# Hymba block on one NeuronCore: gate products a chunk ahead, VectorE's extra work behind the level copies, the output gate beside the square, other fillers

## The chip, the cores and the metric

The kernel runs on one NeuronCore of a Trainium2 chip. Its engines are TensorE (PE in the profile, its weight loads PEld), VectorE (DVE), ScalarE (ACT) and GpSimd (POOL); every transfer is issued from SyncE's queue (SP). The metric is device time in microseconds of one launch. Before the change the median of three runs is 1251.34 us (1251.17 to 1252.57).

## The reference, cut to what matters

One layer runs over 1024 tokens (and 16 meta tokens ahead of them) of width 1024: a norm, one input projection, three head groups side by side (stick-breaking attention, a Mamba-2 SSD, HGRN2), an output projection, and a squared-ReLU MLP. The change concerns the two recurrent groups, which the reference runs in chunks of 128 tokens:

```python
def ssd step(state, inp):                      # per chunk, 8 heads of 64
    decay = masked_decay(acum_t - acum_s)      # exp, causal
    y_diag = einsum('btsh,bshp->bthp', (c_c b_c) * decay, x_c)
    y_off  = einsum('bthn,bhpn->bthp', c_h, state) * exp(acum)
    state  = state * exp(acum[-1]) + einsum('bshn,bsh,bshp->bhpn', b_h, w_end, x_c)
    ...
def hgrn2 step(S, inp):                        # per chunk, 4 heads of 64
    gcum = cumsum(g_c, axis=1)                 # g = log forget gate, per channel
    scores  = einsum('bthk,btshk,bshk->btsh', q_c, masked_decay(gcum_t - gcum_s), k_c)
    o = einsum('btsh,bshv->bthv', scores, v_c) + einsum('bthk,bhkv->bthv', q_c * exp(gcum), S)
    S = S * exp(gcum[-1]) + einsum('bshk,bshv->bhkv', k_c * exp(gcum[-1] - gcum), v_c)
...
o = rmsnorm(o, out_norm) * silu(g)             # the output gate
h = h + concat([o_sb, o_ssd, o_hg]) @ w_out
```

## The kernel before

The launch has four stretches: the input projection and attention (to about 388 us of the profiled execution), chunks 1 to 8 of the two recurrences (to about 621 us), and the MLP as two levels of block products, to the end.

The function chunk(c, steps, per) does one chunk. HGRN2's scores are not made with logarithms but in seven levels, block sizes b = 1, 2, 4, ... 64. The tile qb holds the queries, kx the keys (cx in the profile, one ring of buffers), f4 the forget gates, S the scores (a5 or wT, read as a). In level b hg_levels issues on TensorE two products of all keys with the later half of each block pair's queries (pa<-qb,cx; four records in the profile); on VectorE the multiplication of that query half by the gate product of the earlier half (qb<-qb,f) and a predicated copy of the new scores into S; on GpSimd the multiplication of the earlier key half by the gate product of the later half (cx<-cx,f), and then the product of the pairs of gates, in place, as the gates of the next level (f<-f). Level b+1's score product therefore waits for both halves. In even chunks the query and gate tiles are slices of one g buffer, so the names there are g<-g,g and cx<-cx,g.

Between the levels stands the SSD's work: on VectorE two scans of the decay (levels 1 and 2), y = state output by decay (wT<-mq,cwt, third level), the decays times c b (k<-pb,k, 128x512 each, fourth and fifth), and the scaling of the state (sst<-sst,tot); on GpSimd the 128x512 products a<-a,dtt (third level), a<-a,dbc (fourth), wT<-wT,a (fifth) and a<-a,cwt (sixth).

TensorE is filled up with the products of the output projection of the chunk before, out_steps(c-1), 48 matmuls of 128x512 in two halves (mf<-g,wsA or wsB): take(steps, per) issues per of them after each level, one after the diagonal product (pb<-a,k), and what is left ahead of the transposes at the chunk's end. Chunk 1 fills with work of the gates (ig_all), chunk 8 with the output projection of chunk 7 and first products of the MLP. In chunks 3 to 6 a normalised tile of the MLP is made as well.

The chunk's end: VectorE adds the HGRN2 output (cx<-pc,cx; otf in the code), ScalarE squares it, VectorE sums (ro<-cx, a TENSOR_REDUCE), GpSimd raises the SSD's and HGRN2's mean squares to -1/2 (rr<-rr,mhalf and ro<-ro,mhalf), VectorE multiplies by it (cx<-cx,ro), GpSimd multiplies by the output gate (cx<-cx,igt), and TensorE transposes the mix: attention's part (pc<-ident,kto), the SSD's (mq<-ident,wT), HGRN2's (pc<-ident,cx). ScalarE and VectorE split that into two rounded parts for the next output projection. Then the next chunk's first level follows on TensorE.

What sets the order: a scheduler orders each engine's instructions by its own estimate; behind(i, j) adds a dependence without a semaphore, which holds i after j in the queue of one engine. lastcp is the last predicated copy, lastkv the last key product. All loads stand in one queue in the order in which SyncE issues them.

Of the kernel before, what the change touches and what calls it, by code (L numbers as in the profile page):

```python
# [15 lines left out]
P = 128  # L16
# [52 lines left out]
def tile_hybrid_block(  # L69
# [799 lines left out]
    def hg_levels(qb, kx, f4, S, levels, m):  # L869
        for b in levels:  # L870
# [38 lines left out]
    def halves(fn):  # L909
        for h in range(2):  # L910
            fn(slice(64 * h, 64 * h + 64), h)
# [55 lines left out]
    def mlp_tr(c, xn, qq=(0, 1), tag="mf"):  # L967

        off = (c - 1) * P
        for q in qq:  # L970
# [2 lines left out]
            urgent[0] = A.copy(hi, src)  # L973
            V.tensor_tensor(lo, src, hi, op=ALU.subtract)

    def chunk(c, steps, per):

        t0 = (c - 1) * P
# [6 lines left out]
        if c <= 2:
            if c == 1:
                hgt[1] = sb([4, P], "qb"), sb([4, P], "f4"), sb([4, P], "a5")
            else:
                qf = sb([G3], "g3")[:, 0:D].rearrange("p (a q t) -> p a q t", a=2, t=P)
                hgt[0] = qf[:, 0], qf[:, 1], sb([4, P], "wT")  # L990
            halves(lambda s, h: G.memset(hgt[c % 2][0][s, 1 - h::2, :], 0.0))
            G.memset(hgt[c % 2][2], 0.0)
        qb, f4, S = hgt[c % 2]
        halves(lambda s, h: SY.dma_start(qb[s, h::2, :], dr_qf[:, s, cs].rearrange("f p t -> p f t")))
        kx = sb([CU], "cu")[:, 0:256].rearrange("p (q t) -> p q t", t=P)
        SY.dma_start(kx, dr_k[:, :, cs].rearrange("f p t -> p f t"))
        for h in range(2):
            SY.dma_start(f4[:, h::2, :], dr_f[:, :, cs].rearrange("f p t -> p f t"))
        xb = sb([K4], "k4")[:, 0:D].rearrange("p (f t) -> p f t", t=P)
        SY.dma_start(xb, dr_x[:, :, cs].rearrange("f p t -> p f t"))  # L1000
        dec = sb([K4], "k4")[:, 0:D].rearrange("p (h t) -> p h t", t=P)
# [12 lines left out]
        yf = y.rearrange("p h d -> p (h d)")  # L1014
        ot = sb([3 * P], "ca")[:, 0:256].rearrange("p (h d) -> p h d", d=64)
        for n, b in enumerate(LEVELS):
            hg_levels(qb, kx, f4, S, (b,), P)
            if n <= 1:
                dg = dec[:, 4 * n:4 * n + 4, :].rearrange("p h t -> p (h t)")
                behind(V.tensor_tensor_scan(dg, dg, ident4, 0.0, ALU.mult, ALU.add), lastcp[0])  # L1020
            if n == 0:
                xt = ssd_x(xb, P)
            elif n == 1:
                bt = ssd_b(xb, P)
            elif n == 2:
                pc = ps("pb")
                for g in range(2):
                    mm(pc[:, g * P:(g + 1) * P], lhsT=xb[:, 4 + g, :], rhs=xb[:, 6 + g, :], start=True, stop=True)
                py = ps("mq")
                for g in range(2):  # L1030
                    mm(py[:, g * 256:(g + 1) * 256], lhsT=xb[:, 6 + g, :], rhs=sst[:, g * 256:(g + 1) * 256],
                       start=True, stop=True)
                V.tensor_tensor(y, py.rearrange("p (h d) -> p h d", d=64), inner(cwt[:, c, 0, :], [P, 8, 64]),
                                op=ALU.mult)
                behind(G.tensor_tensor(xd, xt, inner(dtt[:, c, :], [P, 8, 64]), op=ALU.mult), lastkv[0])
            elif n in (3, 4):
                g = n - 3
# [562 lines left out]
```

## Time and profile before

| | us |
|---|---|
| three runs, median (range) | 1251.34 (1251.17 to 1252.57) |
| the profiled execution's own time | 1251.57 |
| its span, first to last instruction | 1249.5 |
| TensorE busy, share of the span | 1209.6, 97% |
| VectorE, ScalarE, GpSimd busy | 885.8, 584.0, 429.9 |
| chunks 1 to 8, about | 388 to 621 |

The profile is of one execution of the program. A row of the timeline gives the start of an instruction, its duration, the engine, the operation with output and inputs (128x512 is partitions by elements), and in square brackets how long the engine had stood idle before it and who released it. A count (x4) says that so many alike were joined in a row. Matmuls overlap in their pipeline, so ends are modelled. PEclk, or granted clock, is the clock that the throttle gave TensorE as a share of full speed.

### The profile page before, as it was taken

What the parts mean: (1) busy time and instruction counts of PE and PEld (TensorE: products, weight loads), DVE (VectorE), ACT (ScalarE), POOL (GpSimd) and SP (SyncE); (2) the same over time, 40 slices, a digit from 0 to 9 for tenths busy, and PEclk for the clock granted to TensorE, in tenths of its full rate; (3) what the DMA queues carried; (4) which work ended last, traced back from release to release, by engine and by line L of the source; (5) the groups of instructions that cost most, each with busy time, mean ns of one, the idle gap of its engine ahead of it and who ended that gap; (6) DMA issues with size and microseconds to landing.
All of it is one profiled execution on the core that took longest, in us unless ns stands there. A gap on an engine that the chain in (4) does not pass through costs nothing.

```text
span 1249.5 us, 18592 instructions
## 1 busy us (share of the span) xinstructions
PE 1209.6 (97%) x6362; PEld 1037.4 (83%) x6362; DVE 885.8 (71%) x1449; ACT 584.0 (47%) x1237; POOL 429.9 (34%) x500
## 2 busy tenths in 40 slices
PE   7999999999999998998899999999999999999998
PEld 6989999999888777777788888888887888888887
DVE  5777877775324688887546756666998778778777
ACT  6755676664322332233355644445566444344331
POOL 4233222322102466766524555666752000000000
PEclk9999999999999989999999999999999999999999
DMA  6311112233345666463246666777766554554556
GB/s 209 94 40 46 54 39 58 71 97 99 85 118 132 177 206 133 94 121 92 70 143 188 224 210 215 241 242 245 233 210 215 174 157 138 161 152 148 163 190 211
DMA packets 195031, 184.14 MB, mean 147 GB/s; under 512 B 14405, under 2 KB 149853, under 8 KB 194938
## 3 DMA queue, kind: packets, MB, share of 16 engines
q1 hardware_dynamic: 194938, 182.97, 48.9%
q8 instruction: 50, 0.82, 0.3%
q14 instruction: 43, 0.35, 0.1%
HBM read 128.25 MB, written 54.67 MB: 146 GB/s over the span
## 4 chain that ended last, share of the span: by engine, by line
PE 78%; DVE 9%; POOL 3%; ACT 3%; issue 3%; DMA 3%; SPq 0%; POOLq 0%; ACTq 0%; DVEq 0%
PE pa L119 25%; PE mf L119 23%; PE pc L119 17%; PE mq L119 7%; PE pb L119 3%; DVE k L96 3%; DVE g L96 2%; PE pb L122 1%; POOL cx L96 1%; DVE a L96 1%; PE pa L122 1%; DVE cx L96 1%; DVE wT L96 1%; PE pc L122 1%; ACT g L96 1%
## 5 line engine op out<-in xcount | busy, mean ns | idle before, releaser
L119 PE MATMUL pa<-g,k 128*128 128x512 f32 x864 | 208.8, 389 | 0.8 <-DVE f L96 0.8
L119 PEld LDWEIGHTS pa<-g,k 128*128 128x128 f32 x864 | 162.0, 188 | 35.2 <-DVE f L96 1.2
L119 PE MATMUL mf<-g,wsA 128*128 128x384 f32 (+2 forms) x624 | 139.3, 358 | 0.0
L119 PE MATMUL mf<-g,wsB 128*128 128x384 f32 (+2 forms) x624 | 136.5, 355 | 0.0
L119 PEld LDWEIGHTS mf<-g,wsA 128*128 128x128 f32 x624 | 104.4, 190 | 6.6 <-DVE wsA L96 0.3
L119 PEld LDWEIGHTS mf<-g,wsB 128*128 128x128 f32 x624 | 103.6, 189 | 6.1
L96 DVE TENSOR_TENSOR k<-g,k 128x512 fp32r<-128x512 f32 x80 | 81.0, 1013 | 28.6 <-ACT k L96 28.0
L119 PE MATMUL mf<-g,g 128*128 128x512 f32 (+1 forms) x408 | 100.8, 394 | 0.0
L96 ACT CAST g<-cx 128x512 fp32r<-128x512 f32 x80 | 49.5, 619 | 85.8 <-DVE cx L96 59.2
L119 PEld LDWEIGHTS mf<-g,g 128*128 128x128 f32 (+1 forms) x408 | 72.5, 183 | 15.1 <-issue 0.3
L119 PE MATMUL pc<-g,k 128*128 128x512 f32 x336 | 82.5, 389 | 0.0
L96 DVE TENSOR_TENSOR g<-pa,g 128x512 f32<-128x512 f32 (+2 forms) x82 | 54.9, 679 | 38.1 <-PE pa L119 32.2
L96 POOL TENSOR_TENSOR cx<-cx 128x384 f32<-128x384 f32 (+2 forms) x34 | 38.6, 1135 | 118.7 <-ACT cx L96 78.6
L119 PEld LDWEIGHTS pc<-g,k 128*128 128x128 f32 x336 | 63.1, 188 | 13.2
L119 PE MATMUL mf<-g,k 128*128 128x512 f32 x288 | 69.6, 392 | 1.8 <-ACT a L96 1.5
L119 PE MATMUL pa<-g,st 128*128 128x512 f32 x240 | 65.1, 390 | 0.3 <-ACT g L96 0.3
L119 PEld LDWEIGHTS mf<-g,k 128*128 128x128 f32 x288 | 53.6, 188 | 13.5 <-ACT a L96 1.9
L96 DVE TENSOR_TENSOR g<-cx,g 128x512 fp32r<-128x512 f32 x80 | 60.5, 756 | 4.9 <-ACT g L96 3.5
L96 POOL TENSOR_TENSOR g<-g,g 128x512 f32<-128x512 f32 x32 | 45.7, 1436 | 49.8 <-issue 45.5
L96 ACT CAST k<-g 128x512 fp32r<-128x512 f32 x80 | 48.9, 615 | 20.2 <-PE pb L119 11.4
L119 PEld LDWEIGHTS pa<-g,st 128*128 128x128 f32 x240 | 45.0, 188 | 10.1 <-ACT g L96 0.7
L96 DVE SCALAR_TENSOR_TENSOR cx<-cx,cwb 128x384 f32<-128x384 f32 (+1 forms) x72 | 43.5, 605 | 9.2 <-ACT cx L96 8.6
(358 smaller groups left out, 2719.6 us busy)
## 6 DMA issues: line engine op xcount, KB each, us to landing
g<-in_w_up_dram SPq DMA_DIRECT2D x48, 512.0 KB, 4.9
st<-in_w_in_dram SPq DMA_DIRECT2D x51, 256.0 KB, 2.9
cx<-in_w_down_dram SPq DMA_DIRECT2D x48, 256.0 KB, 2.8
wT<-dr_s SPq DMA_DIRECT2D x45, 256.0 KB, 3.0
dr_s<-a SPq DMA_DIRECT2D x40, 256.0 KB, 2.3
g<-in_x_dram SPq DMA_DIRECT2D x16, 512.0 KB, 5.5
dr_s<-st SPq DMA_DIRECT2D x32, 256.0 KB, 2.5
a<-dr_s SPq DMA_DIRECT2D x23, 256.0 KB, 2.9
```

The lines of the kernel that those rows point to most:

```text
L96: i = fn(*a, **k)
L119: return queue(nc.tensor.matmul(*a, **k))
L122: return queue(nc.tensor.transpose(*a, **k))
```

## The change

Five things are changed in the chunks. The gates of chunk c+1 are loaded during chunk c (load_f), and their products of all levels are written to a tile of their own, fp, a chunk ahead, one level behind each key product of the running chunk (f_products); chunk 1's seven products stand before its levels, and hg_level reads f4 or fp. Three VectorE products of the SSD (y, the decays times c b, the scaling of the state) are held behind the predicated copy of their level, and the addition to the state behind the row sum. The output gate is multiplied in on GpSimd beside ScalarE's square, before the two powers, and VectorE's multiplication by the norm is the last step ahead of the transposes. Before the transposes at most 10 filler matmuls are taken instead of all that is left, so that two follow behind them; chunk 2 takes 6 per level instead of 5. The DMA scratch of the program is made smaller, which gives the room for fp.

```diff
+    def f_products(f4, fp, b):
+        v = f_level(f4, fp, b).rearrange("p q (n t) -> p q n t", t=2)
+        return G.tensor_tensor(f_level(f4, fp, 2 * b), v[:, :, :, 0], v[:, :, :, 1], op=ALU.mult)
...
+    def load_f(c):
+        cs = slice(NM + (c - 1) * P, NM + c * P)
...
+        f4 = hgt[c % 2][1]
+        for h in range(2):
+            SY.dma_start(f4[:, h::2, :], dr_f[:, :, cs].rearrange("f p t -> p f t"))
...
+        if c == 1:
+            load_f(1)
+            for b in LEVELS:
+                f_products(hgt[1][1], hgt[1][3], b)
+        qb, f4, S, fp = hgt[c % 2]
...
-        for h in range(2):
-            SY.dma_start(f4[:, h::2, :], dr_f[:, :, cs].rearrange("f p t -> p f t"))
+        if c < 8:
+            load_f(c + 1)
...
-            hg_levels(qb, kx, f4, S, (b,), P)
+            hg_level(qb, kx, f4, fp, S, n)
+            if c < 8:
+                behind(f_products(hgt[1 - c % 2][1], hgt[1 - c % 2][3], b), lastkv[0])
...
-                V.tensor_tensor(y, py.rearrange("p (h d) -> p h d", d=64), inner(cwt[:, c, 0, :], [P, 8, 64]),
-                                op=ALU.mult)
+                behind(V.tensor_tensor(y, py.rearrange("p (h d) -> p h d", d=64), inner(cwt[:, c, 0, :], [P, 8, 64]),
+                                       op=ALU.mult), lastcp[0])
...
-                V.tensor_tensor(dec[:, 4 * g:4 * g + 4, :], outer(pc[:, g * P:(g + 1) * P], [P, 4, P]),
-                                dec[:, 4 * g:4 * g + 4, :], op=ALU.mult)
+                behind(V.tensor_tensor(dec[:, 4 * g:4 * g + 4, :], outer(pc[:, g * P:(g + 1) * P], [P, 4, P]),
+                                       dec[:, 4 * g:4 * g + 4, :], op=ALU.mult), lastcp[0])
...
-        V.reduce_sum(ro[:, 0:4], sq.rearrange("p (h d) -> p h d", d=64), axis=mybir.AxisListType.X)
+        red = V.reduce_sum(ro[:, 0:4], sq.rearrange("p (h d) -> p h d", d=64), axis=mybir.AxisListType.X)
+        gated = ig[:, 256:512]
+        G.tensor_tensor(gated, otf, gated, op=ALU.mult)
...
-        V.tensor_tensor(ot, ot, inner(ro[:, 0:4], [P, 4, 64]), op=ALU.mult)
-        G.tensor_tensor(otf, otf, ig[:, 256:512], op=ALU.mult)
+        V.tensor_tensor(ot, gated.rearrange("p (h d) -> p h d", d=64), inner(ro[:, 0:4], [P, 4, 64]), op=ALU.mult)
...
-        V.tensor_tensor(s3, s3, inner(tot[:, c - 1, :], [P, 8, 64]), op=ALU.mult)
-        V.tensor_tensor(sst, pst, sst, op=ALU.add)
+        behind(V.tensor_tensor(s3, s3, inner(tot[:, c - 1, :], [P, 8, 64]), op=ALU.mult), lastcp[0])
+        behind(V.tensor_tensor(sst, pst, sst, op=ALU.add), red)
...
-        take(steps, 1000 if c < 8 else 26)
+        take(steps, 10 if c < 8 else 26)
...
-        chunk(c, under(out_steps(c - 1), wo1, 0, 5), 5)
+        chunk(c, under(out_steps(c - 1), wo1, 0, 5), 6 if c == 2 else 5)
...
-    nc = _bacc.Bacc("TRN2", target_bir_lowering=False, num_devices=1)
+    nc = _bacc.Bacc("TRN2", target_bir_lowering=False, num_devices=1, dynamic_dma_scratch_size=1024)
```

The order of VectorE in chunk 5, from the third level's query half to the fifth level's copy, is this before (qb is the query tile, a the scores, k the decays, wT the SSD's output, sst its state):

```order
L96 TENSOR_TENSOR qb_4203<-qb_4203,f_568_4204 128x64x4
L96 COPY_PREDICATED a_569_4205<-hmask,pa_5329 128x64x4
L96 TENSOR_TENSOR k_740_5279<-pb_5336,k_740_5279 128x512 x2
L96 TENSOR_TENSOR wT_5288<-mq_5339,cwt 128x512
L96 TENSOR_TENSOR sst<-sst,tot 128x512
L96 TENSOR_TENSOR qb_4203<-qb_4203,f_568_4204 128x32x8
L96 COPY_PREDICATED a_569_4205<-hmask,pa_5349 128x32x8
L96 TENSOR_TENSOR qb_4203<-qb_4203,f_568_4204 128x16x16
L96 COPY_PREDICATED a_569_4205<-hmask,pa_5371 128x16x16
L96 TENSOR_TENSOR g_749_5304<-mf_5306,g_749_5304 128x512
```

and this after:

```order
L96 TENSOR_TENSOR qb_4203<-qb_4203,fp_4206 128x64x4
L96 COPY_PREDICATED a_569_4205<-hmask,pa_5340 128x64x4
L96 TENSOR_TENSOR wT_5299<-mq_5350,cwt 128x512
L96 TENSOR_TENSOR qb_4203<-qb_4203,fp_4206 128x32x8
L96 COPY_PREDICATED a_569_4205<-hmask,pa_5360 128x32x8
L96 TENSOR_TENSOR k_742_5290<-pb_5347,k_742_5290 128x512
L96 TENSOR_TENSOR qb_4203<-qb_4203,fp_4206 128x16x16
L96 COPY_PREDICATED a_569_4205<-hmask,pa_5382 128x16x16
L96 TENSOR_TENSOR k_742_5290<-pb_5347,k_742_5290 128x512
L96 TENSOR_TENSOR g_751_5315<-mf_5317,g_751_5315 128x512
```

Between the copies of the third level and the query half of the fourth stand one product instead of four; the two decay products are behind the copies of the fourth and the fifth level, and the state's scaling stands behind the seventh level's copy.

GpSimd in the same place, from the third level's key product on (cx is the keys, a and wT the SSD's tiles), before:

```order
L96 TENSOR_TENSOR cx<-cx,f_568_4204 128x32x4
L96 TENSOR_TENSOR a_743_5286<-a_748_5302,dtt 128x512
L96 TENSOR_TENSOR f_568_4204<-f_568_4204 128x64
L96 TENSOR_TENSOR cx<-cx,f_568_4204 128x16x8
L96 TENSOR_TENSOR a_748_5302<-a_748_5302,dbc 128x512
L96 TENSOR_TENSOR f_568_4204<-f_568_4204 128x32
L96 TENSOR_TENSOR cx<-cx,f_568_4204 128x8x16
L96 TENSOR_TENSOR wT_5288<-wT_5288,a_748_5302 128x512
```

and after:

```order
L96 TENSOR_TENSOR cx<-cx,fp_4206 128x32x4
L96 TENSOR_TENSOR fp_4224<-fp_4224 128x4x16
L96 TENSOR_TENSOR a_745_5297<-a_750_5313,dtt 128x512
L96 TENSOR_TENSOR cx<-cx,fp_4206 128x16x8
L96 TENSOR_TENSOR fp_4224<-fp_4224 128x4x8
L96 TENSOR_TENSOR a_750_5313<-a_750_5313,dbc 128x512
L96 TENSOR_TENSOR cx<-cx,fp_4206 128x8x16
L96 TENSOR_TENSOR fp_4224<-fp_4224 128x4x4
L96 TENSOR_TENSOR wT_5299<-wT_5299,a_750_5313 128x512
```

The products stand in the queue as many times as before, now those of the next chunk's gates (fp_4224) and ahead of the SSD's product of the level instead of behind it; the key products read fp_4206, which the chunk before has written.

GpSimd at the end of chunk 5, from the clearing of the query tile on (rr and ro are the mean squares, igt the output gate), before:

```order
L96 MEMSET g_621_4553 64x2x128
L96 TENSOR_SCALAR rr_5205<-rr_5205 128x2
L96 TENSOR_TENSOR rr_5205<-rr_5205,mhalf 128x2
L96 TENSOR_SCALAR ro_5222<-ro_5222 128x4
L96 TENSOR_TENSOR ro_5222<-ro_5222,mhalf 128x4
L96 TENSOR_TENSOR cx<-cx,igt_5043 128x256
```

and after:

```order
L96 MEMSET g_571_4222 64x2x128
L96 TENSOR_TENSOR igt_5054<-cx,igt_5054 128x256
L96 TENSOR_SCALAR rr_5216<-rr_5216 128x2
L96 TENSOR_TENSOR rr_5216<-rr_5216,mhalf 128x2
L96 TENSOR_SCALAR ro_5233<-ro_5233 128x4
L96 TENSOR_TENSOR ro_5233<-ro_5233,mhalf 128x4
```

The gate has moved from the last place of the five to the first.

## Rows read from the trace of the kernel before

**Rows 1.** The view of the cores: span, and mean granted clock of TensorE.

```profile
core 0: 1249.5 us, clock 0.997
```

**Rows 2.** The table by stretch, of which chunk 2, chunk 5 and chunk 8 are shown: stretch and its length, busy time and instructions of PE, PEld, DVE, ACT and POOL, granted clock, DMA share, GB/s.

```profile
429.00:461.00 32.00, 26.76 (x140) 21.78 (x139) 26.21 (x43) 10.04 (x23) 18.13 (x26) 0.89 0.70 234
...
512.00:538.00 26.00, 23.70 (x146) 20.11 (x147) 21.38 (x38) 7.84 (x17) 17.79 (x28) 1.00 0.49 107
...
589.00:621.00 32.00, 28.40 (x162) 23.75 (x163) 19.84 (x35) 12.00 (x31) 18.77 (x31) 1.00 0.26 87
```

**Rows 3.** The waits of TensorE from 386 to 621 us, all chunks, without the last line of 0.3 us: what it waited for, us in total, how many times, the longest.

```profile
PE pa L119 <- DVE g L96: 5.2, 5, 1.3
PE pa L119 <- DVE qb L96: 4.6, 3, 1.9
PE pc L122 <- POOL cx L96: 3.3, 6, 0.7
PE pa L119 <- POOL cx L96: 2.8, 7, 0.5
PE pb L119 <- ACT a L96: 2.7, 1, 2.7
PE mf L119 <- ACT a L96: 1.5, 1, 1.5
```

**Rows 4.** TensorE's timeline in chunk 5 from the fourth level on (fillers and other products between are left out).

```profile
519.73 0.61 PE L119 MATMUL pa<-qb,cx 128*128 128x128 f32 x4
...
522.78 0.68 PE L119 MATMUL pa<-qb,cx 128*128 128x128 f32 x4 [1.28 <-DVE qb L96]
...
524.46 0.60 PE L119 MATMUL pa<-qb,cx 128*128 128x128 f32 x4
...
526.50 0.71 PE L119 MATMUL pa<-qb,cx 128*128 128x128 f32 x4
...
533.36 3.12 PE L119 MATMUL mf<-g,wsB 128*128 128x512 f32 x12
...
537.75 0.44 PE L122 MATMUL pc<-ident,cx 128*128 128x128 f32 x2 [0.62 <-POOL cx L96]
```

**Rows 5.** VectorE's timeline in chunk 5.

```profile
518.91 1.28 DVE L96 TENSOR_TENSOR k<-pb,k 128x512 f32<-128x512 f32 x2
520.11 0.68 DVE L96 TENSOR_TENSOR wT<-mq,cwt 128x512 f32<-128x512 f32 x1
520.70 0.75 DVE L96 TENSOR_TENSOR sst<-sst,tot 128x512 f32<-128x512 f32 x1
521.38 1.26 DVE L96 TENSOR_TENSOR qb<-qb,f 128x256 f32<-128x256 f32 x1
...
525.76 0.43 DVE L96 TENSOR_TENSOR qb<-qb,f 128x256 f32<-128x256 f32 x1 [0.63 <-POOL f L96]
...
533.02 0.42 DVE L96 TENSOR_TENSOR cx<-pc,cx 128x256 f32<-128x256 f32 x1
...
534.58 0.41 DVE L96 TENSOR_REDUCE ro<-cx 128x4 f32<-128x256 f32 x1
536.40 0.43 DVE L96 TENSOR_TENSOR cx<-cx,ro 128x256 f32<-128x256 f32 x1 [1.41 <-POOL ro L96]
```

**Rows 6.** GpSimd's timeline in chunk 5.

```profile
520.48 0.42 POOL L96 TENSOR_TENSOR cx<-cx,f 128x128 f32<-128x128 f32 x1 [0.54 <-PE pa L119]
520.87 1.49 POOL L96 TENSOR_TENSOR a<-a,dbc 128x512 f32<-128x512 f32 x1
522.72 0.31 POOL L96 TENSOR_TENSOR f<-f 128x32 f32<-128x32 f32 x1 [0.36 <-DVE qb L96]
523.61 0.66 POOL L96 TENSOR_TENSOR cx<-cx,f 128x128 f32<-128x128 f32 x1 [0.58 <-PE pa L119]
524.24 1.28 POOL L96 TENSOR_TENSOR wT<-wT,a 128x512 f32<-128x512 f32 x1
...
525.80 0.65 POOL L96 TENSOR_TENSOR cx<-cx,f 128x128 f32<-128x128 f32 x1
526.41 1.04 POOL L96 TENSOR_TENSOR a<-a,cwt 128x512 f32<-128x512 f32 x1
...
533.93 0.19 POOL L96 TENSOR_SCALAR rr<-rr 128x2 f32<-128x2 f32 x1 [1.56 <-ACT a L96]
...
535.36 1.01 POOL L96 TENSOR_TENSOR ro<-ro,mhalf 128x4 f32<-128x4 f32 x1
536.97 0.72 POOL L96 TENSOR_TENSOR cx<-cx,igt 128x256 f32<-128x256 f32 x1 [0.60 <-DVE cx L96]
```

**Rows 7.** TensorE's timeline in chunk 2, at its third level.

```profile
436.89 1.22 PE L119 MATMUL pb<-k 128*128 128x128 f32 x4 [2.71 <-ACT a L96]
...
439.90 2.69 PE L119 MATMUL mf<-g,wsA 128*128 128x512 f32 x5
...
444.94 1.40 PE L119 MATMUL mf<-g,wsA 128*128 128x512 f32 x5
```

**Rows 8.** ScalarE's timeline in chunk 2, ahead of the row of TensorE that waits.

```profile
435.04 1.33 ACT L96 ACTIVATE g<-g,nwt 128x512 fp32r<-128x512 f32 x2 [4.94 <-DMA g<-in_w_out_dram]
```

**Rows 9.** TensorE's timeline, the fifth and the seventh level of chunk 8.

```profile
599.87 0.68 PE L119 MATMUL pa<-g,cx 128*128 128x128 f32 x4 [1.29 <-DVE g L96]
...
603.60 0.71 PE L119 MATMUL pa<-g,cx 128*128 128x128 f32 x4 [0.29 <-POOL cx L96]
```

More of the change, by code (lines that the diff above doesn't have):

```diff
@@ L53 @@
 BUFS = dict(g1=4, g2=2, g3=8, wsA=1, wsB=1, k4=4, st=3, a1=1, a2=1, a3=1, a4=1, a5=1, qb=1, f4=1, wT=2,
-            igt=1, rr=6, ro=2, sm=4, sst=1)
+            igt=1, rr=6, ro=2, sm=4, sst=1, fp=2)
 PBUFS = dict(mf=2, mq=1, pa=2, pb=1, pc=2)
@@ L892, in hg_levels, with f_level, hg_level @@
                 G.tensor_tensor(fv[:, :, :, 0, 0], fv[:, :, :, 0, 0], fv[:, :, :, 1, 0], op=ALU.mult)
+    FP = {2: 0, 4: 64, 8: 96, 16: 112, 32: 120, 64: 124, 128: 126}
+    def f_level(f4, fp, b):
+        return f4 if b == 1 else fp[:, :, FP[b]:FP[b] + P // b]
+    def f_products(f4, fp, b):
+        v = f_level(f4, fp, b).rearrange("p q (n t) -> p q n t", t=2)
+        return G.tensor_tensor(f_level(f4, fp, 2 * b), v[:, :, :, 0], v[:, :, :, 1], op=ALU.mult)
+    def hg_level(qb, kx, f4, fp, S, li):
+        b = LEVELS[li]
+        n = 64 // b
+        kv, qv, sv = (t.rearrange("p q (n t b) -> p q n t b", t=2, b=b) for t in (kx, qb, S))
+        fv = f_level(f4, fp, b).rearrange("p q (n t) -> p q n t", t=2)
+        pl = ps("pa")
+        for p in range(2):
+            mm(pl[:, p * P:(p + 1) * P], lhsT=kx[:, p, :], rhs=qv[:, 2 * p:2 * p + 2, :, 1, :], start=True, stop=True)
+        lq = V.tensor_tensor(qv[:, :, :, 1, :], qv[:, :, :, 1, :], fv[:, :, :, 0:1].broadcast_to([P, 4, n, b]),
+                             op=ALU.mult)
+        msk = hmask[:, li:li + 1, :].broadcast_to([P, 4, 64]).rearrange("p q (n b) -> p q n b", b=b)
+        lastcp[0] = V.copy_predicated(sv[:, :, :, 1, :], msk, pl[:, 0:256].rearrange("p (q n b) -> p q n b", q=4, b=b))
+        behind(lastcp[0], lq)
+        lastkv[0] = G.tensor_tensor(kv[:, :, :, 0, :], kv[:, :, :, 0, :],
+                                    fv[:, 0::2, :, 1:2].broadcast_to([P, 2, n, b]), op=ALU.mult)
     def hg_tokens(kx, m):
@@ L974, in mlp_tr @@
             V.tensor_tensor(lo, src, hi, op=ALU.subtract)
+    def load_f(c):
+        cs = slice(NM + (c - 1) * P, NM + c * P)
+        if c <= 2:
+            if c == 1:
+                hgt[1] = sb([4, P], "qb"), sb([4, P], "f4"), sb([4, P], "a5"), sb([4, P], "fp")
+            else:
+                qf = sb([G3], "g3")[:, 0:D].rearrange("p (a q t) -> p a q t", a=2, t=P)
+                hgt[0] = qf[:, 0], qf[:, 1], sb([4, P], "wT"), sb([4, P], "fp")
+            halves(lambda s, h: G.memset(hgt[c % 2][0][s, 1 - h::2, :], 0.0))
+            G.memset(hgt[c % 2][2], 0.0)
+        f4 = hgt[c % 2][1]
+        for h in range(2):
+            SY.dma_start(f4[:, h::2, :], dr_f[:, :, cs].rearrange("f p t -> p f t"))
     def chunk(c, steps, per):
@@ L982, in chunk @@
         mixes[c] = mix
[L985 to L993, printed above, removed]
+        if c == 1:
+            load_f(1)
+            for b in LEVELS:
+                f_products(hgt[1][1], hgt[1][3], b)
+        qb, f4, S, fp = hgt[c % 2]
         halves(lambda s, h: SY.dma_start(qb[s, h::2, :], dr_qf[:, s, cs].rearrange("f p t -> p f t")))
@@ L1091, in chunk @@
         rms_r(ro, P, 4)
-        V.tensor_tensor(ot, ot, inner(ro[:, 0:4], [P, 4, 64]), op=ALU.mult)
-        G.tensor_tensor(otf, otf, ig[:, 256:512], op=ALU.mult)
+        V.tensor_tensor(ot, gated.rearrange("p (h d) -> p h d", d=64), inner(ro[:, 0:4], [P, 4, 64]), op=ALU.mult)
         pst = ssd_state(bt, xw, P)
         s3 = sst.rearrange("p (h d) -> p h d", d=64)
-        V.tensor_tensor(s3, s3, inner(tot[:, c - 1, :], [P, 8, 64]), op=ALU.mult)
-        V.tensor_tensor(sst, pst, sst, op=ALU.add)
+        behind(V.tensor_tensor(s3, s3, inner(tot[:, c - 1, :], [P, 8, 64]), op=ALU.mult), lastcp[0])
+        behind(V.tensor_tensor(sst, pst, sst, op=ALU.add), red)
         hv = hst.rearrange("p a h d -> p a (h d)")
-        V.tensor_tensor(hv, hv, f4[:, 0::2, 0:1].broadcast_to([P, 2, P]), op=ALU.mult)
+        V.tensor_tensor(hv, hv, fp[:, 0::2, FP[P]:FP[P] + 1].broadcast_to([P, 2, P]), op=ALU.mult)
         halves(lambda s, h: V.tensor_tensor(hst[s, :, h, :], pk[s, 0:2, h, :], hst[s, :, h, :], op=ALU.add))
-        take(steps, 1000 if c < 8 else 26)
+        take(steps, 10 if c < 8 else 26)
         p2 = ps("pc")
```

## The prediction

> **What bounds the kernel now.** First the cores: one core, 1249.5 us, granted clock 0.997 [rows 1], so nearly all of the time is at full clock, and the profiled execution of 1251.57 us is 0.23 above the median of 1251.34. Then the stretches: the change touches chunks 1 to 8 alone, and there TensorE is busy for 23.70 of 26 us in a middle chunk, VectorE for 21.38 and GpSimd for 17.79 [rows 2]. TensorE is the bound, so an edit pays only where it takes away a wait of TensorE; the fillers keep their number. The waits of TensorE over all the chunks are the ceiling: 5.2 + 4.6 + 3.3 + 2.8 + 2.7 + 1.5 = 20.1 us [rows 3], 1.6% of the time. Two groups are large: scores that wait for VectorE's query half (9.8 us in 8 waits) and the transposes at a chunk's end that wait for GpSimd's gate (3.3 in 6).
>
> The middle chunks are alike, so I walk through chunk 5, with the fourth level's scores, at 519.73, as zero. The fifth level stands at 3.05, the sixth at 4.73, the seventh at 6.77, and the last transposes at 18.02 [rows 4]. The fifth comes after a wait of 1.28. Its releaser is the query half of 1.26 us, which started at 521.38, 1.65 after the scores that let it go; ahead of it in VectorE's queue stood the two decay products (1.28 for both), y (0.68) and the state's scaling (0.75) [rows 5]. At the end GpSimd finishes the second power at 535.36 + 1.01 = 536.37, VectorE multiplies for 0.43, GpSimd puts the gate in for 0.72, and TensorE goes on at 537.75, after a wait of 0.62 [rows 4 to 6].
>
> **The change part by part. VectorE behind the copies.** Only y (0.68) is left ahead of the fourth query half; its input comes from a product ahead of the fourth scores, so it hides there. The query half then starts with its scores, and alone it takes 0.43, not 1.26 [rows 5]. Two waits are thus gone, and the fifth level can stand at 3.05 − 1.28 = 1.77, which is TensorE's own work, and the sixth at 1.77 + 1.68 = 3.45, the seventh at 3.45 + 2.04 = 5.49 by the distances of before, in which nothing waits [rows 4]. VectorE's next extras: each decay product (0.64) now follows a copy, and VectorE stood idle for 0.63 ahead of the sixth query half [rows 5]; the state's scaling (0.75) follows the seventh copy, where its hiding place is the diagonal product on TensorE. I cost these at nothing; without that cover they are rival C.
>
> **GpSimd is late next.** Its fourth key product ends at 0.75 + 0.42 = 1.17; a gate product of 0.31 follows, now ahead of the SSD's product and no longer held by VectorE (0.36 idle before); then a<-a,dbc. It took 1.49 beside the long query half; the same shape took 1.04 as a<-a,cwt [rows 6]. I take 1.04, since the query half that it ran beside moves off: 2.52. The fifth key product (0.66) ends at 3.18, ahead of the sixth scores at 3.45. Product 0.31, wT<-wT,a 1.28, key product 0.65: 5.42 [rows 6], against 5.49 on TensorE. Five joints of some 0.03 to 0.05 between instructions put it at about 5.65, so GpSimd holds the seventh level by 0.1 to 0.2: 6.77 − 5.65 = 1.1 gained, of 1.28. The third level's wait on GpSimd (within the 2.8 us of [rows 3]) I leave as it is: the products still stand between the key products there.
>
> **Gate products a chunk ahead.** They are as many and as long as before, and no longer between two levels of one chain; their gain is the 0.36 and the wait of 0.63 above, already in the sum. Chunk 8 has none to make: both its waits, 1.29 and 0.29 [rows 9], can go: 1.6. The loads move ahead in SyncE's queue by a chunk; they are small and land long before they are read.
>
> **Output gate beside the square.** From the second power on, the path is now VectorE's 0.43 and the transposes: the gate's 0.72 and a joint of some 0.1 go, 0.8 less. Paid for ahead: GpSimd's gate can start when VectorE's otf is there, 533.02 + 0.42 = 533.44, and ends at 534.16, while rr was ready at 533.93 [rows 5, 6]: 0.2 to 0.4 later for the powers that follow. Net 0.5, at most the 0.62 of the wait.
>
> **Fillers.** Two matmuls move behind the last transposes, 3.12 / 12 = 0.26 each [rows 4]. They cover nothing of TensorE ahead of the next scores, and 0.5 less cover stands ahead of the transposes; with the waits before them mostly gone I count 0.2 lost. A middle chunk so gains 1.1 + 0.5 − 0.2 = 1.4; bounds 0.6 (GpSimd at its long durations) and 2.3 (all its waits).
>
> **Chunks 1 and 2.** Here the order changes most: seven gate products of chunk 2 now stand at chunk 1's end on GpSimd, ahead of the two powers: between seven of the short row of 0.31, 2.2, and seven of the gate's 0.72, 5.0 [rows 6]; I take 3, since each is half as long as the one before; six fillers a level instead of five in chunk 2. What sets chunk 2 is another thing: its third level waits 2.71 for ScalarE [rows 7], which itself stands 4.94 for the output weights [rows 8], at 435.04. These weights' issue moves hardly, so a later end of chunk 1 is mostly absorbed. Bounds: −4 (all of the 2.7 and the first-levels' waits go) and +3 (the products come out whole). Nearest is the row that stays, the weights' landing: I take −0.5.
>
> **Sum.** Chunks 3 to 6: 4 × 1.4 = 5.6. Chunk 7, which makes no MLP tile but has the longest wait, 1.9 [rows 3]: 1.3 (its end gains less, as the next chunk's queue is shorter). Chunk 8: 1.6, and 0.3 by the gate: 1.9. Chunks 1 and 2: 0.5. Together 9.3, under half of the 20.1. The profiled execution would be 1251.57 − 9.3 = 1242.3, a median 1242.0.
>
> **The rivals. B, GpSimd becomes the pace.** a<-a,dbc stays at 1.49 instead of 1.04 and the key products at 0.66 instead of 0.42: 0.45 + 0.24 = 0.69 later in a middle chunk, of which the slack leaves 0.6. For it: the 1.49 and the 0.66 are the rows at that very place [rows 6], and VectorE stays as busy there as before, with the decays. Against it: the decay products read one input from PSUM. Then a middle chunk gains 0.8, chunk 7 0.7, chunk 8 1.4: 3.2 + 0.7 + 1.4 + 0.5 = 5.8, a time of 1245.5. Beside it stands the Trainium skill, GPSIMD Engine Reference, "8. Key points": GpSimd shares its SBUF interfaces with VectorE and contends with it when VectorE runs in a two-port mode or reads two SBUF inputs. By that rule, the trace agrees: a query half and a GpSimd product that run together took 1.26 and 1.49, apart 0.43 and 1.04.
>
> **C, slower: VectorE becomes the bound at the end.** The decays, and the state's scaling, 1.28 + 0.75, with y 0.68 2.7 in all, find no idle VectorE in the levels and come out behind the seventh copy, ahead of the additions that the diagonal product releases. It decides from the point where VectorE's idle time in levels 5 to 7 is under what was moved there. Price: 2.7 − 1.28 = +1.4 a chunk in five chunks, 7.0, less 1.9 in chunk 8 and 0.5: 1251.3 + 4.6 = 1255.9. Against it: 4.6 us of VectorE idle in a middle chunk (26 − 21.38 [rows 2]), with 0.63 ahead of the sixth query half alone.
>
> **D, the half clock of chunk 2 goes.** Five fillers took 2.69 at 439.90 and 1.40 at 444.94 [rows 7]; the mean of the stretch was 0.89 [rows 2], so 0.11 × 32 = 3.5 us were lost to 1.2 GHz after the wait of 2.71. If that wait closes, 3.5 more: 1238.5. Against it: the weights land when they landed.
>
> **E, no change to speak of.** GpSimd as in B, and chunk 2's seven products delay chunk 1's end and with it the transposes, 3 us, with nothing of it absorbed: −5.8 + 0.5 + 3 = −2.3, a time of 1249.0.
>
> **How the numbers follow.** A measurement of this kernel can tell about 0.2%, 2.5 us, from no change. Forecast 0.53 (1240 to 1244), B 0.25, D 0.07, all faster: 0.85. E 0.09: the same. C 0.06: slower. The time is the likeliest case's, 1242.0. The range reaches down to D and up to the worse end of B, and leaves out C, E and what lies beyond D, 0.2 in all: 1237.8 to 1248.3.
>
> **What would show it.** Right: in chunks 3 to 7 the fifth scores come without a wait of over 0.3, the fourth query half lasts some 0.43 and starts with its scores; the seventh scores stand about 5.6 after the fourth; the last transposes follow VectorE's cx<-igt,ro and no GpSimd row; what took 26 us in chunk 5 takes 24.6. B shows as a GpSimd row of 1.4 to 1.5 ahead of scores that wait for cx; C as a diagonal product's addition on VectorE that starts late; D as a granted clock of 1.0 in chunk 2; E as a chunk 1 that is 3 us longer. It would be wrong altogether if the scores in chunks 3 to 6 waited for something that no row here shows, such as a late load of gates.

## The result, and the profile after

| | before | after |
|---|---|---|
| median of four runs, us | 1251.95 (1251.17 to 1252.76) | 1240.29 (1239.97 to 1243.86) |
| ratio, 95% interval | | 0.9908 (0.9897 to 0.9920) |
| the profiled execution, us (span) | 1251.57 (1249.5) | 1243.86 (1242.1) |

Some 11.6 us less, 0.9%; 1242.0 was forecast, with 1237.8 to 1248.3 as the range.

The profiled execution of after is 3.5 us or more above the others: it reaches chunk 1 2.7 us later than before, in a stretch where both kernels run the same order, with 3.4 us at half clock (granted clock 0.5) near 62 us, so chunks are compared by their own lengths.

TensorE's starts of the first-level scores (the first pa<-..,cx of a chunk; chunk 8 to the first transpose pa<-ident,qb behind it) give the length of each chunk, us:

| chunk | 1 | 2 | 3 | 4 | 5 | 6 | 7 | 8 | sum |
|---|---|---|---|---|---|---|---|---|---|
| before | 38.40 | 31.76 | 25.62 | 25.83 | 25.77 | 25.80 | 25.41 | 37.28 | 235.87 |
| after | 40.33 | 29.82 | 24.22 | 24.29 | 24.27 | 24.27 | 23.33 | 35.22 | 225.75 |
| forecast of the difference | −0.5 for both | | −1.4 | −1.4 | −1.4 | −1.4 | −1.3 | −1.9 | −9.3 |
| measured | +1.93 | −1.94 | −1.40 | −1.54 | −1.50 | −1.53 | −2.08 | −2.06 | −10.12 |

The waits of TensorE from 386 to 621 us, after; they answer to [rows 3]: what it waited for, total, times, longest.

```profile
PE pa L119 <- DVE g L96: 3.4, 2, 2.0
PE pc L122 <- DVE cx L96: 2.4, 6, 0.5
PE mq L122 <- ACT wT L96: 1.7, 2, 1.2
PE mf L119 <- ACT a L96: 1.3, 1, 1.3
PE pa L119 <- POOL cx L96: 0.6, 2, 0.4
```

The 9.8 us of waits for VectorE's query half have become 3.4, in two waits, both in chunk 2. The ends of chunks still wait, now for VectorE's multiplication, 2.4 in all instead of 3.3.

TensorE's timeline in chunk 5, after, against [rows 4]: the scores of levels 4 to 7, the transposes of the MLP tile between the last two of them, the fillers and transposes at the end, and the next chunk's first scores.

```profile
519.41 0.60 PE L119 MATMUL pa<-qb,cx 128*128 128x128 f32 x4
...
521.01 0.61 PE L119 MATMUL pa<-qb,cx 128*128 128x128 f32 x4
...
522.61 0.67 PE L119 MATMUL pa<-qb,cx 128*128 128x128 f32 x4
...
523.92 0.63 PE L122 MATMUL mf<-ident,k 128*128 128x128 f32 x4 [0.17 <-DVE g L96]
...
525.09 0.61 PE L119 MATMUL pa<-qb,cx 128*128 128x128 f32 x4
...
531.84 2.66 PE L119 MATMUL mf<-g,wsB 128*128 128x512 f32 x10
...
535.53 0.44 PE L122 MATMUL pc<-ident,cx 128*128 128x128 f32 x2 [0.38 <-DVE cx L96]
535.72 0.71 PE L119 MATMUL mf<-g,wsB 128*128 128x512 f32 x2
536.27 0.62 PE L119 MATMUL pa<-g,cx 128*128 128x128 f32 x4
```

Counted from the fourth scores, the fifth stand at 1.60, the sixth at 3.20, the seventh at 5.68 (before 3.05, 4.73, 6.77; for the seventh 5.65 was forecast), the last transposes at 16.12 (18.02).

VectorE and then GpSimd in the same place, after, against [rows 5] and [rows 6].

```profile
520.05 0.43 DVE L96 TENSOR_TENSOR qb<-qb,fp 128x256 f32<-128x256 f32 x1 [0.91 <-PE pa L119]
...
523.10 0.67 DVE L96 TENSOR_TENSOR g<-mf,g 128x512 f32<-128x512 f32 x1
```

```profile
520.16 0.59 POOL L96 TENSOR_TENSOR cx<-cx,fp 128x128 f32<-128x128 f32 x1 [0.39 <-PE pa L119]
520.73 0.23 POOL L96 TENSOR_TENSOR fp<-fp 128x32 f32<-128x32 f32 x1
520.92 1.03 POOL L96 TENSOR_TENSOR a<-a,dbc 128x512 f32<-128x512 f32 x1
521.93 0.59 POOL L96 TENSOR_TENSOR cx<-cx,fp 128x128 f32<-128x128 f32 x1
...
523.90 0.58 POOL L96 TENSOR_TENSOR cx<-cx,fp 128x128 f32<-128x128 f32 x1
...
531.85 0.73 POOL L96 TENSOR_TENSOR igt<-cx,igt 128x256 f32<-128x256 f32 x1 [0.99 <-DVE cx L96]
```

The fourth query half takes 0.43 and is released by its scores, 0.64 behind their start; a<-a,dbc takes 1.03. The key products come in time: the one for the seventh scores ends at 523.90 + 0.58 = 524.48, 0.61 ahead of the scores at 525.09. What stands just ahead of those are the transposes of the MLP tile, which wait for VectorE's g<-mf,g; they start 0.89 behind the fillers in front of them, 0.55 in the kernel before.

Chunk 1's end on GpSimd, after: the products of chunk 2's gates, which start when those have landed, the gate, and the two powers behind.

```profile
425.52 1.09 POOL L96 TENSOR_TENSOR fp<-g 128x256 f32<-128x256 f32 x1 [2.85 <-DMA g<-dr_f]
426.69 1.15 POOL L96 TENSOR_TENSOR fp<-fp 128x128 f32<-128x128 f32 x3
...
428.29 0.50 POOL L96 TENSOR_TENSOR fp<-fp 128x16 f32<-128x16 f32 x2
428.75 0.73 POOL L96 TENSOR_TENSOR igt<-cx,igt 128x256 f32<-128x256 f32 x1
...
430.26 0.70 POOL L96 TENSOR_TENSOR rr<-rr,mhalf 128x2 f32<-128x2 f32 x1
430.95 1.01 POOL L96 TENSOR_TENSOR ro<-ro,mhalf 128x4 f32<-128x4 f32 x1
```

TensorE waits 1.24 there for the SSD's scaled output. In chunk 2 its third level then waits 2.04, for a query half queued behind a split of the output weights. ScalarE's first split of these starts 44.6 us behind chunk 1's first scores, in the kernel before 44.4 ([rows 8]): the weights land as late as before. The half clock in chunk 2 lasts 3.4 us instead of 6.8.

### The profile page after: what moved, and what is told of

Same layout as the page of the kernel before. It is cut to its first block, busy times and chain, and to the rows that moved or that the text cites. A ratio compares the mean times of both kernels' runs of the same rounds, so it can differ in the third digit from the quotient of the medians.

```text
span 1242.1 us, 18593 instructions
## 1 busy us (share of the span) xinstructions
PE 1210.7 (97%) x6362; PEld 1037.9 (84%) x6362; DVE 880.5 (71%) x1449; ACT 584.2 (47%) x1237; POOL 424.5 (34%) x500
## 4 chain that ended last, share of the span: by engine, by line
PE 80%; DVE 8%; issue 3%; ACT 3%; POOL 3%; DMA 3%; SPq 0%; DVEq 0%; POOLq 0%; ACTq 0%
PE pa L119 25%; PE mf L119 25%; PE pc L119 16%; PE mq L119 7%; PE pb L119 3%; DVE g L96 3%; DVE k L96 2%; PE pb L122 1%; POOL rr L96 1%; PE pa L122 1%; ACT k L96 1%; DVE cx L96 1%; DMA g<-in_x_dram 1%; DMA g<-in_w_out_dram 1%; DVE a L96 1%
## 5 line engine op out<-in xcount | busy, mean ns | idle before, releaser
L119 PEld LDWEIGHTS pa<-g,st 128*128 128x128 f32 x240 | 45.0, 188 | 10.1 <-ACT g L96 0.8
```

What stands on the lines that cost most here:

```text
L119: return queue(nc.tensor.matmul(*a, **k))
```

## The experiments

Each was timed against the kernel before on the same chip (the change in the runs above). An interval on a ratio is about 0.0013 to either side, 1.6 us; finer statements rest on the chunk lengths of the profiled execution, which mostly agree to 0.05 us between kernels with the same order in the chunk. The last two columns are such lengths, in us.

| kernel | us | ratio (interval) | chunks 3 to 6 | chunk 7 |
|---|---|---|---|---|
| before | 1251.95 to 1252.91 | 1 | 25.62 to 25.83 | 25.41 |
| the change | 1240.29 | 0.9908 (0.9897, 0.9920) | 24.22 to 24.29 | 23.33 |
| e_dve_unheld | 1244.03 | 0.9933 (0.9920, 0.9945) | 24.23 to 24.24 | 26.70 |
| e_gate_last | 1246.17 | 0.9955 (0.9942, 0.9969) | 24.61 to 24.64 | 23.72 |
| e_fillers_old | 1238.10 | 0.9891 (0.9877, 0.9904) | 23.78 to 23.80 | 22.68 |
| e_dve_only | 1246.34 | 0.9954 (0.9940, 0.9967) | 24.47 to 24.70 | 23.78 |
| e_products_only | 1241.44 | 0.9909 (0.9893, 0.9924) | 24.05 to 24.13 | 25.19 |
| e_product_behind | 1245.42 | 0.9941 (0.9929, 0.9954) | 25.02 to 25.05 | 25.36 |
| e_products2_late | 1242.37 | 0.9918 (0.9905, 0.9932) | 24.23 to 24.30 | 23.35 |
| v_splits_later | 1233.81 | 0.9854 (0.9840, 0.9867) | 23.59 to 24.14 | 22.68 |
| v_spread | 1232.75 | 0.9851 (0.9836, 0.9866) | 23.57 to 23.59 | 22.67 |
| v_spread_late2 | 1234.56 | 0.9855 (0.9839, 0.9872) | 23.58 to 24.14 | 22.66 |

**e_dve_unheld**, from the changed kernel:

```diff
-                behind(V.tensor_tensor(y, ...), lastcp[0])
+                V.tensor_tensor(y, ...)
-                behind(V.tensor_tensor(dec[:, 4 * g:4 * g + 4, :], ...), lastcp[0])
+                V.tensor_tensor(dec[:, 4 * g:4 * g + 4, :], ...)
-        behind(V.tensor_tensor(s3, ...), lastcp[0])
-        behind(V.tensor_tensor(sst, pst, sst, op=ALU.add), red)
+        V.tensor_tensor(s3, ...)
+        V.tensor_tensor(sst, pst, sst, op=ALU.add)
```

> The changed kernel with VectorE's y, decay products, state scaling and state addition not held behind the copies, so that they stand ahead of the fourth query half again; all else as changed. Theory (VectorE's order gives the levels' gain): the fifth scores wait 1.2 to 1.3 us again in chunks 3 to 8, the seventh scores stand some 6.8 after the fourth instead of 5.7; 6 x 1.1 = 6.6 us, a time near 1247. Rival (the gate products a chunk ahead give the gain): the waits stay away, 1240 to 1242.

Neither came out whole. The queue ahead of the fourth query half was the old one again, yet the wait of the fifth scores came back at 0.48 only and chunks 3 to 6 kept their length: in exchange TensorE gets back 0.4 between the sixth and the seventh scores, and the wait of 0.38 at the chunk's end is gone. TensorE, VectorE and GpSimd, chunk 5 of e_dve_unheld:

```profile
517.95 0.68 PE L119 MATMUL pa<-qb,cx 128*128 128x128 f32 x4 [0.48 <-DVE qb L96]
```

```profile
516.56 0.86 DVE L96 TENSOR_TENSOR sst<-sst,tot 128x512 f32<-128x512 f32 x1
517.35 0.46 DVE L96 TENSOR_TENSOR qb<-qb,fp 128x256 f32<-128x256 f32 x1
```

```profile
516.84 0.68 POOL L96 TENSOR_TENSOR fp<-fp 128x32 f32<-128x32 f32 x1
517.49 1.22 POOL L96 TENSOR_TENSOR a<-a,dbc 128x512 f32<-128x512 f32 x1
```

The query half starts 0.14 ahead of a<-a,dbc and takes 0.46. In chunk 7, where one more VectorE instruction stands ahead of it, it comes second:

```profile
566.47 1.26 DVE L96 TENSOR_TENSOR qb<-qb,fp 128x256 f32<-128x256 f32 x1
```

```profile
565.96 1.48 POOL L96 TENSOR_TENSOR a<-a,dbc 128x512 f32<-128x512 f32 x1
```

There it takes 1.26, TensorE waits 1.93, and chunk 7 has 3.4 us at half clock just behind: 26.70 against 23.33. In these profiles that is more than the whole difference of the chunks, 2.8. Part of it can be the half clock of this execution: one execution of e_dve_unheld had a mean clock of 1.000 and took 1241.39, and the one of the change with that clock 1240.21.

**e_dve_only**: the kernel before with the lines just shown as + put in as they stand in the change, no more.

> The kernel before with only VectorE's three extras held behind the copies (and the state's addition behind the row sum); gate products in place, gate last, fillers as before. Theory: the fifth scores' wait goes and GpSimd with its products in place is just in time for the sixth and the seventh: 1.0 to 1.2 a chunk in six chunks, 6 to 7 us, a time of 1245 to 1246. Rival (without the products a chunk ahead GpSimd holds the sixth and seventh scores, so the order of VectorE alone brings little): the seventh scores stay over 6.3 behind the fourth, 1248 to 1250.

The theory held: chunk 5 is 24.68 instead of 25.77, 1.1 less, the seventh scores stand 6.00 after the fourth (6.77), and GpSimd, products in place, is just in time. So the order of VectorE alone does take the wait away. Of the 1.1 some 0.5 comes at the chunk's end, where the transposes wait 0.24 instead of 0.62. Chunk 2 is longer here, 33.20 instead of 31.76.

**e_products_only**: the kernel before with load_f, f_products, hg_level and the scratch size of the diff, no more.

> The kernel before with the gates' loads and products a chunk ahead alone (and the smaller DMA scratch that makes their room); VectorE's extras, the gate and the fillers as before. The prediction's step (the fifth wait is VectorE's order, so the products alone leave it at 1.28): chunks 3 to 6 stay at 25.4 to 25.8 us, 1250 to 1252. Theory after the first runs (a query half that starts while GpSimd's 128x512 product runs takes 1.26 instead of 0.45; a product ahead of that one starts it later, so the query half comes first): the fifth wait is 0.3 to 0.5, chunks 3 to 6 are 24.0 to 24.4 us, 1243 to 1245.

The prediction's step fell: the products alone bring 1.6 to 1.7 a chunk in chunks 3 to 6, and 0.9909 in all, which nothing here tells from the 0.9908 of the whole change. VectorE's four products stand ahead of the fourth query half as before; it starts 0.14 ahead of a<-a,dbc and takes 0.45:

```profile
517.89 0.45 DVE L96 TENSOR_TENSOR qb<-qb,fp 128x256 f32<-128x256 f32 x1
```

```profile
518.03 1.22 POOL L96 TENSOR_TENSOR a<-a,dbc 128x512 f32<-128x512 f32 x1
```

That explains half: the fifth scores wait 0.48 instead of 1.28. The other 0.87 comes between the seventh scores and the next chunk, where the transposes no longer wait for the gate, though it is last as before. VectorE there, first in the kernel before, whose diagonal product (pb<-a,k) starts at 528.65:

```profile
527.66 0.43 DVE L96 TENSOR_TENSOR qb<-qb,f 128x256 f32<-128x256 f32 x1 [0.55 <-POOL f L96]
528.34 1.13 DVE L96 TENSOR_TENSOR g<-st,g 128x512 fp32r<-128x512 f32 x1
...
531.37 0.68 DVE L96 TENSOR_TENSOR wT<-pb,wT 128x512 f32<-128x512 f32 x1
```

and in e_products_only, where it starts at 524.26:

```profile
522.86 0.46 DVE L96 TENSOR_TENSOR qb<-qb,fp 128x256 f32<-128x256 f32 x1 [0.31 <-PE pa L119]
523.57 0.71 DVE L96 TENSOR_TENSOR g<-st,g 128x512 fp32r<-128x512 f32 x1
...
526.26 0.69 DVE L96 TENSOR_TENSOR wT<-pb,wT 128x512 f32<-128x512 f32 x1
```

The seventh query half no longer waits for GpSimd's gate product, g<-st,g is shorter, and the SSD's addition follows the diagonal product's start by 2.00 instead of 2.72; all that leads from it to the gate is as much earlier. Which of the two does more was not tried.

**e_product_behind**, from e_dve_unheld:

```diff
-            if c < 8:
+            if c < 8 and n != 3:
                 behind(f_products(hgt[1 - c % 2][1], hgt[1 - c % 2][3], b), lastkv[0])
...
-                    behind(G.tensor_tensor(xt, xt, inner(dbc[:, 2, :], [P, 8, 64]), op=ALU.mult), lastkv[0])
+                    xp = G.tensor_tensor(xt, xt, inner(dbc[:, 2, :], [P, 8, 64]), op=ALU.mult)
+                    behind(xp, lastkv[0])
+                    if c < 8:
+                        behind(f_products(hgt[1 - c % 2][1], hgt[1 - c % 2][3], b), xp)
```

> As e_dve_unheld (VectorE's order as before, the rest as changed), and GpSimd's gate product of the fourth level stands behind its 128x512 product a<-a,dbc, as it did before, instead of ahead. Theory (who starts first decides): a<-a,dbc starts some 0.7 earlier, ahead of the query half, which takes 1.2 us again; the fifth wait goes from 0.48 to 1.2 to 1.3 in chunks 3 to 6, 25.0 us each instead of 24.24, 3 us in all over e_dve_unheld. Rival (the wait of 0.48 is VectorE's queue alone, and the other 0.8 was the product in place): 0.48 stays, and the time is that of e_dve_unheld.

The theory held closely, with one instruction moved behind its neighbour; it takes 0.68 ahead of it and 0.42 behind. VectorE, GpSimd and TensorE in chunk 5:

```profile
517.18 1.26 DVE L96 TENSOR_TENSOR qb<-qb,fp 128x256 f32<-128x256 f32 x1
```

```profile
516.67 1.49 POOL L96 TENSOR_TENSOR a<-a,dbc 128x512 f32<-128x512 f32 x1
518.12 0.42 POOL L96 TENSOR_TENSOR fp<-fp 128x32 f32<-128x32 f32 x1
```

```profile
518.59 0.68 PE L119 MATMUL pa<-qb,cx 128*128 128x128 f32 x4 [1.28 <-POOL fp L96]
```

a<-a,dbc starts first, and the query half ends 0.28 behind its end: 517.18 + 1.26 = 518.44 against 518.16, and in the kernel before 522.64 against 522.36 [rows 5, 6]. The wait is 1.28 again, chunks 25.0. The row names fp, which ended last and which the scores don't read; they follow the query half by 0.15, before by 0.14. In time the kernel lies 1.4 above e_dve_unheld, not 3: in the profiled execution chunks 2 and 7 ran wholly at full clock and are 2.5 shorter.

**e_gate_last**: the changed kernel with the lines of the gate as before.

> The changed kernel with the output gate back behind VectorE's multiplication by the norm; all else as changed. Theory: the last transposes wait for GpSimd's gate again, 0.5 to 0.8 us in each of chunks 2 to 7 more than now, 3 to 5 us together, a time of 1243 to 1245. Rival (the gate was hidden, and ahead of the powers it delays as much as it saves): within 1 us of the changed kernel's 1240.3.

```profile
536.68 0.44 PE L122 MATMUL pc<-ident,cx 128*128 128x128 f32 x2 [0.79 <-POOL cx L96]
```

The transposes wait 0.79 for GpSimd instead of 0.38 for VectorE, a middle chunk is 24.62 instead of 24.27: beside ten fillers the gate's place is worth 0.35 a chunk. (In e_products_only, with the gate last and twelve fillers, the transposes of chunks 3 to 6 show no wait.) The whole is 5.9 slower by the ratios, give or take some 2; its chunks account for 4.0, of which 2.0 are chunk 2, with 6.8 us at half clock there instead of 3.4.

**e_fillers_old**: the changed kernel with take(steps, 1000 if c < 8 else 26) and 5 in chunk 2.

> The changed kernel with the fillers as before: 5 per level in chunk 2, and all that is left ahead of the transposes. Theory (two fillers behind the transposes cost 0.2 a chunk as cover and bring nothing): 1239 to 1240. Rival (they cover the splitting of the mix and the first levels' waits): the third level's wait on GpSimd of 0.4 comes back in chunks 3 to 7, and the time is 1242 to 1243.

The theory held, with more than it expected: 23.79 instead of 24.27 a middle chunk. The third level's wait of 0.4 does come back, as the rival had it, but the fourth scores stand hardly later in the chunk than with ten fillers (7.46 against 7.41 behind the first); nearly the whole difference lies at the end. Its end of chunk 5 on TensorE:

```profile
529.38 3.10 PE L119 MATMUL mf<-g,wsB 128*128 128x512 f32 x12
...
533.09 0.44 PE L122 MATMUL pc<-ident,cx 128*128 128x128 f32 x2
533.36 0.62 PE L119 MATMUL pa<-g,cx 128*128 128x128 f32 x4
```

Twelve fillers cover VectorE's last step; with ten TensorE waits 0.38 for it and does the two afterwards.

**e_products2_late**, from the changed kernel:

```diff
-            if c < 8:
+            if 1 < c < 8:
                 behind(f_products(hgt[1 - c % 2][1], hgt[1 - c % 2][3], b), lastkv[0])
...
         rms_r(ro, P, 4)
+        if c == 1:
+            for b in LEVELS:
+                behind(f_products(hgt[0][1], hgt[0][3], b), rms_last[0])
```

> The changed kernel with chunk 2's seven gate products behind chunk 1's last power on GpSimd instead of ahead of its powers. Theory (the delay of chunk 1's end is absorbed by the wait for the output weights in chunk 2): chunk 1 is 38.4 to 39 us instead of 40.3, chunk 2 longer by nearly as much, the time within 0.7 of the changed kernel's. Rival (it is on the path): 1.3 to 1.9 less.

Chunk 1 falls from 40.33 to 39.04 and chunk 2 grows from 29.82 to 31.56. Its third level waits 3.23 instead of 2.04 and stands 46.8 us behind chunk 1's first scores, in the change 46.9: absorbed, as forecast. The rest of chunk 2's growth goes with 6.8 us at half clock instead of 3.4. The two times differ by less than their intervals.

**v_splits_later**, from e_fillers_old; the weights' splits are drawn at other fillers, and ScalarE keeps them behind the last copy of ssd_b:

```diff
+            steps = at(out_steps(1), wo1, (0, 10, 13, 16, 19, 22, 25, 28, 31, 34))
...
-        A.copy(bt[:m, 0:256], pb[:m, 0:256])
+        i = A.copy(bt[:m, 0:256], pb[:m, 0:256])
+        urgent[0] = i
```

> As e_fillers_old (the changed kernel with the fillers as before), and in chunk 2 the splitting of the output weights on ScalarE and VectorE is taken at the 10th filler and later and stands on ScalarE behind the copies of the SSD's transposes. Theory (chunk 2's third level waits only because the copies are queued behind a split that waits for the weights' transfer): chunk 2 goes from 30.4 to 25.5 to 27 us, the stretch at half clock goes with the wait, 3 to 5 us less than e_fillers_old. Rival (the weights are needed then anyway, or other loads land as late): the wait moves to the second half's fillers or to the loads, less than 1 us gained.

Chunk 2 goes from 30.40, with 3.4 us at half clock, to 26.79, and in the profiled execution no stretch of the launch but its end runs at half clock; 4.3 us less than e_fillers_old, 6.5 less than the change. ScalarE and TensorE in chunk 2:

```profile
432.58 0.37 ACT L96 COPY cx<-mq 128x256 f32<-128x256 f32 x1 [1.25 <-PE mq L122]
434.68 5.39 ACT L96 ACTIVATE g<-g,nwt 128x512 fp32r<-128x512 f32 x8 [1.72 <-DMA g<-in_w_out_dram]
```

```profile
434.37 0.61 PE L119 MATMUL pb<-k 128*128 128x128 f32 x4
```

The copies are out before the weights land, and the third level runs through; in the kernel before, the row pb<-k waited 2.71 [rows 7], in e_fillers_old 2.26.

**v_spread** draws the splits at fillers (0, 10, 15, 20, 24, 28, 31, 34, 37); **v_spread_late2** adds the late products of e_products2_late.

> As v_splits_later, with the splits of the output weights in chunk 2 spread over more fillers (the 10th, 15th, 20th, 24th, 28th, 31st, 34th, 37th), so that one or two instead of two or three of VectorE's parts stand between two levels. Theory (the waits of 1.49, 0.92 and 1.56 in chunk 2 are VectorE's split parts ahead of the query halves): chunk 2 goes from 26.8 to 25 to 26 us, 1 to 2 us less in all. Rival (the splits are needed by the second half's fillers and only move the wait to them): no gain.

> As v_spread, and chunk 2's gate products behind chunk 1's last power. Theory (now that chunk 2 no longer waits for the weights at its third level, what chunk 1's end loses to the seven products is on the path): chunk 1 is 38.4 instead of 39.0, some 0.5 us less in all. Rival (chunk 2's first key product or levels wait for the late products instead): no gain or up to 1 us lost.

v_spread: chunk 2 is 27.24, no shorter. The waits of 1.49, 0.92 and 1.56 became 0.30 and 2.20, and behind the second the clock is halved for 3.4 us, which v_splits_later did not have. No gain, as the rival said, but not by its reason: the wait is not at the second half's fillers but at the seventh scores, whose query half still stands behind two parts of a split in a row (1.83 us from 440.47 on). v_spread_late2: chunk 1 is 38.39, as expected, but chunk 2 waits at the seventh level all the same and has 10.2 us at half clock: 30.79, in a profiled execution of 1238.38, the slowest of its four. No gain to be told. The three, 1.5% under the kernel before, are the fastest; nothing here separates them.

## Why the prediction was right, and where not

**The bound and the sum** held: −9.3 forecast, −10.1 by chunks, −11.6 by medians. Up to 1.7 of either can be the half clock in chunk 2, 3.4 us shorter, as D describes in part. B did not come: a<-a,dbc took 1.03, and the key products 0.59, near B's 0.66, with nothing late for it.

**The seventh scores at 5.68 were luck.** The 5.65 was GpSimd's time. GpSimd was ready at 5.07, 0.6 earlier, and in chunk 7, which makes no MLP tile, the scores follow its key product at 5.12. In chunks 3 to 6 the tile's transposes hold them: VectorE's g<-mf,g, for which these wait, now stands behind a decay product. The step "I cost these at nothing" left that out: from the sixth to the seventh scores it is 2.48 instead of 2.04, and 2.05 again in e_dve_unheld, where the decay products are not held. So GpSimd was put 0.6 too slow and VectorE's hold 0.4 too cheap, and the two nearly cancel.

**The mechanism of the wait was half right.** The step that failed is that of the gate products a chunk ahead, "their gain is the 0.36 and the wait of 0.63 above, already in the sum". Products alone bring 1.7 a middle chunk, 0.8 of it the fifth wait and 0.9 the chunk's end; VectorE's order alone brings 1.1, and in the change it adds nothing to the products there. The 1.28 us were not the queue's length alone: 0.48 was that, and 0.80 that the query half was issued while GpSimd's product ran, ended just behind it and grew from 0.45 to 1.26 us (e_product_behind gives exactly this back). Either edit changes who starts first: VectorE's hold starts the query half 0.64 behind its scores instead of 1.65, the gate product starts a<-a,dbc 1.78 behind them instead of 1.14. In the change as a whole the hold shortens chunk 7 alone. The prediction had both durations and named contention under B, but let the long query half hang on VectorE's queue alone, and left out that a product put ahead of a<-a,dbc also changes which of the two starts first. The Trainium skill, GPSIMD Engine Reference, "8. Key points", says that GpSimd shares its SBUF interfaces with VectorE and contends with VectorE's instructions that have two SBUF inputs, as the query half has; the trace agrees, with 1.26 us against 0.45.

**The gate**: 0.5 forecast, 0.35 measured beside ten fillers. **The fillers**: −0.2 forecast, −0.48 measured, because the wait that was to vanish stayed at 0.38 with ten and is covered by twelve. So the size came out by errors that cancel: 1.1 + 0.5 − 0.2 = 1.4 was forecast, 1.7 + 0.35 − 0.48 = 1.57 is the sum of the parts, 1.50 the whole. The parts are not independent: moving the gate makes good at the chunk's end what moving the fillers loses there, and the products alone are worth as much as all the parts together.

**Chunk 7**: 1.3 forecast, 2.08 measured; its wait of 1.92 goes wholly. **Chunk 8**: 1.9 and 2.06. **Chunks 1 and 2**: −0.5 and 0.0. Chunk 1's end is delayed as E feared, by 1.93 instead of 3, but absorbed; that the weights' landing sets chunk 2 was right, shown by e_products2_late and, the other way round, by v_splits_later. That the gates "land long before they are read" did not hold in chunk 1: GpSimd stood idle for 2.85 until chunk 2's gates had landed.

**C** did not come at its price: the state's scaling behind the seventh copy hid under the diagonal product, and VectorE's end of the chunk is covered by twelve fillers. What stays open: why the half clock of chunk 2 lasts 3.4, 6.8 or 10.2 us in kernels whose waits there differ little, and why chunk 7's wait of 1.93 brought it in the profile of e_dve_unheld and not in that of e_products_only. It also differs between executions of one kernel: the mean granted clock was 0.997, 0.998, 1.000 and 0.998 in the four of the change, so the half clock in a profile is that of one execution.

## What to carry to other kernels

Before moving work off a queue because a short VectorE instruction is long at one place, look at what GpSimd started just ahead of it: one small GpSimd instruction put between can give the same gain. A split that waits for a load, put by a scheduler in front of copies that TensorE needs, cost 3.6 us of one chunk here, the half clock behind it included, more than any other edit gave in a chunk: put such splits behind the copies. Fillers belonged ahead of the last dependent transposes here until these no longer waited. And try each part of a change alone: one of five gave as much as all.

## What was not expected of the hardware

A 128x256 product of VectorE that was issued during a 128x512 product of GpSimd ended 0.28 to 0.29 us after it in the three places shown, 1.26 us long instead of 0.43 to 0.46; issued 0.14 ahead, it was not slowed, and GpSimd's product took 1.22 instead of 1.03. The length is thus no price per instruction: in chunk 5 of the change the fifth query half, issued at 521.66, 0.74 into a<-a,dbc, takes 0.59 and again ends 0.3 behind it.

GpSimd's product waits in the same way: a<-a,dbc ends 0.90 or 0.91 us behind the VectorE product that was issued just ahead of it, behind the state's scaling in chunk 5 of the kernel before (522.36 against 521.45 [rows 5, 6]) as behind the query half in e_dve_unheld (518.71 against 517.81) and e_products_only (519.25 against 518.34). Its 1.49 in the kernel before thus fits the scaling ahead of it, and not the long query half behind it, as the prediction read it.
